# An attention stage with every engine pinned to program order, operands begun three maps ahead, and modulation weights in blocks of 256 features

## The chip, the cores and the metric

The kernel runs on one core of a Trainium2 chip. The metric is the device time of one launch in microseconds, the median of the runs made. A core has five engines that each take their instructions in order: PE (TensorE, matmuls; its weight loads are listed apart as PEld), DVE (VectorE), ACT (ScalarE), POOL (GpSimd) and SP (SyncE, which here only issues DMA transfers). ACT issues a few transfers too.

## What is computed

Two trunk layers over 1152 tokens: 1024 latent tokens and 128 context tokens. Each layer modulates and normalises its input, projects it once, runs four kinds of mixing beside each other, projects the concatenation, and ends with a squared-ReLU MLP:

```python
mod = silu(c) @ ada_w[l] + ada_b[l]              # 6 x 1024 features, for c and for c_ctx
t = mixer_inputs(modulate(x, norm_mix_g, sh1, sc1), lp)
o_a = blocked_attention(...)                     # differential: 4 heads, two maps each, 32-wide q and k
o_a = rmsnorm(o[..., 0, :] - lam * o[..., 1, :], diff_subln_g) * (1 - lam_init)
u   = fourier_mix(t["fnet_u"])
o_c = blocked_attention(...)                     # multi-head latent attention, 4 heads, 96-wide
o_d = blocked_attention(...)                     # grouped queries: 4 q heads, 2 kv heads, 64-wide
x = x + g1 * (concat(o_a, u, o_c, o_d) @ w_out)
x = x + g2 * (square(relu(modulate(x, norm_mlp_g, sh2, sc2) @ mlp_w1)) @ mlp_w2)
```

Latent queries read 1024 latent keys and 128 cached keys in one softmax; context queries read the 128 context keys. All inputs are float32. The kernel keeps that precision by splitting operands into a high and a low part and multiplying the parts.

## The kernel before

**Stages.** Each layer has the same stages in a row: norm and input projection; Fourier mixing, in which the operands of the first attention maps are also read; attention (363 to 871 us in the first layer, 2073 to 2581 us in the second); output projection with the norm before the MLP; and the MLP.

**Maps and pieces.** Attention is 16 maps per layer: maps 0 to 7 differential (two per head), 8 to 11 grouped-query, 12 to 15 latent. `stav` walks a map in ten pieces. For a piece, PE makes scores into a psB buffer (two exist), ACT takes the exponential (L1351) and a float16 copy of it (L1358), POOL subtracts the copy from the exponential for the low part (L294), and `LAG` pieces later PE multiplies the parts by the values into psC. `settle` takes the pieces out of the queue. Beside these matmuls PE makes the row maxima of the following maps (`smax`, into psA, two buffers, reduced by DVE at L1307 and L1312), and the steps of the modulations.

**Operands.** `begin` allocates SBUF pages for a map's operands and issues their loads: for a differential map queries sqr and sqp (96 partitions) and keys sk (97 partitions), for the others gq, gk, mq and mk. There are 44 pages (`NPG`); a load waits until the earlier users of its page are done. Map i+2 is begun when map i starts, its maxima start after those of map i+1 (27 steps, `N_MX`), and `late` loads the second set of operands at column block 5 (`LATE`). When the maxima are known, DVE scales them (L1322), and SP writes the row mr into the last partition of the query tiles by two small transfers (L273).

**Modulations.** `mod_tiles` makes the 6 x 1024 features of ada_w in halves of 512: four loads of ada_p (512 KB each), eight matmuls of 512 columns in two groups, ACT's copy, four matmuls against `quads`, and DVE's additions at L448 and L473. The numbers of steps beside each map are in `MODS`.

**Epilogues.** When a query block's last piece is done, `epi` runs one piece later: DVE divides (L1428 and L1429, or L1437 to L1440). In the second map of a differential head, POOL squares the result (L1502) and DVE sums the squares into dv (L1503); after two heads come the normalisation on POOL and `y_out`, which transposes on PE (L1453), copies on ACT and writes y to DRAM. `y_pairs` reads y back for the output projection and makes high and low parts (L1589, L294).

**What sets the order.** The Tile scheduler orders the instructions of an engine by priorities and expected readiness. Only PE is held to the order in which the attention stage is written (`pin`, while `pinned` is true). DVE, ACT, POOL and SP are ordered by the scheduler, which can also put work of other stages between. Maxima over partitions (`vscale`, `h_scale`) use POOL's `partition_all_reduce`.

## Time and profile before

| | us |
|---|---|
| median of 3 runs | 3513.11 (3511.43 to 3522.86) |
| profiled execution, its own time | 3522.48 |
| its span | 3520.6 |
| PE busy | 3140.4 (89%) |
| DVE busy | 2333.3 (66%) |
| POOL busy | 1486.7 (42%) |
| ACT busy | 1442.1 (41%) |
| mean granted TensorE clock | 0.944 |

The page of the profile shows shares of the span by engine, a strip of 40 slices, the chain of work that ended last, and the costliest groups of instructions. Other views take a stretch of time: the busy time of each engine in it, the list of waits by the instruction that ended them, a timeline of one engine, and the rate of the DMA engines in 40 slices. In the slices the granted clock is 10/10 in the MLP stages and lower in the attention stages.

### The profile page before, as it was taken

To read this page: it belongs to the slowest core of one execution; us is meant where nothing else is said; L and a number is where in the kernel's file an instruction comes from. 1 tells how busy PE (TensorE), PEld (TensorE's weight loads), DVE (VectorE), ACT (ScalarE), POOL (GpSimd) and SP (SyncE) were. 2 spreads that over 40 slices of the span, in tenths; PEclk is the share of its full clock that TensorE was granted. 3 is DMA by queue.
4 is the path that set the end of the run, shared out by engine and by line. 5 is a ranking of instruction groups with operands and counts; after the bars stand their busy time and mean duration, and the time that the engine had idled before them with its cause. 6 is when DMAs were issued, how large, how long until landed. Compare 5 with 4: busy or idle time off the path is not lost.

```text
span 3520.6 us, 59002 instructions
## 1 busy us (share of the span) xinstructions
PE 3140.4 (89%) x23242; PEld 2552.8 (73%) x23242; DVE 2333.3 (66%) x4851; ACT 1442.1 (41%) x2290; POOL 1486.7 (42%) x1146
## 2 busy tenths in 40 slices
PE   7897788988989999999998968887888899999998
PEld 5886566766967777777788856576787776777766
DVE  6865556536377777777687465554446877777776
ACT  4332566745352222222344256665535332222222
POOL 1331576845463323232353146685645422221232
PEclk8998899989999999999999988898999999999999
DMA  6642334434111111111153433433230111111111
GB/s 215 202 145 92 104 123 140 130 113 163 43 49 36 49 49 49 37 48 49 63 183 118 162 94 116 126 112 86 73 132 25 49 48 49 37 49 37 48 37 54
DMA packets 140543, 310.80 MB, mean 88 GB/s; under 512 B 16613, under 2 KB 85682, under 8 KB 140266
## 3 DMA queue, kind: packets, MB, share of 16 engines
q1 hardware_dynamic: 135946, 301.13, 26.6%
q10 hardware_dynamic: 4320, 5.90, 0.5%
q8 instruction: 183, 3.00, 0.4%
q14 instruction: 94, 0.77, 0.1%
HBM read 233.87 MB, written 72.82 MB: 87 GB/s over the span
## 4 chain that ended last, share of the span: by engine, by line
PE 47%; DVE 14%; DMA 13%; issue 11%; POOL 7%; ACT 3%; SPq 1%; POOLq 0%; DVEq 0%; ACTq 0%
PE psD L280 30%; PE psA L280 8%; POOL pg L294 6%; PE psB L280 5%; DVE pg L294 4%; PE psC L280 3%; DMA pg<-sk 2%; DMA pg<-mr 2%; DMA pg<-in_ada_p 2%; DVE pg L1655 2%; DMA pg<-mqp 1%; DMA pg<-sqr 1%; ACT pg L297 1%; SPq L273 1%; DVE pg L1746 1%
## 5 line engine op out<-in xcount | busy, mean ns | idle before, releaser
L280 PE MATMUL psD<-pg,pg 128*128 128x384 f32 (+4 forms) x11173 | 2093.4, 346 | 108.7 <-DVE pg L1784 36.4
L294 POOL TENSOR_TENSOR pg<-pg,pg 128x1024 f16<-128x1024 f32 (+7 forms) x738 | 1216.0, 1663 | 1201.4 <-ACT pg L297 542.4
L280 PEld LDWEIGHTS psD<-pg,pg 128*128 128x128 f32 x8184 | 1422.2, 192 | 77.2 <-DVE pg L294 18.1
L280 PEld LDWEIGHTS <-pg 128*128 128x128 f16 x11448 | 632.3, 101 | 469.0 <-issue 126.0
L1655 DVE SCALAR_TENSOR_TENSOR pg<-psD,mods,pg 128x256 f32<-128x256 f32 (+1 forms) x1088 | 519.5, 511 | 223.0 <-PE psD L280 218.4
L297 ACT ACTIVATE pg<-pg 128x512 f16<-128x512 f32 (+8 forms) x557 | 326.3, 617 | 740.4 <-PE psD L280 312.7
L280 PE MATMUL psA<-pg,pg 128*128 128x128 f16 (+6 forms) x2757 | 497.1, 292 | 92.2 <-DVE mx L1307 19.5
L294 DVE TENSOR_TENSOR pg<-pg,pg 128x384 fp32r<-128x384 f32 (+9 forms) x594 | 472.5, 814 | 62.1 <-ACT pg L297 40.8
L1307 DVE TENSOR_REDUCE mx<-psA 128x1 f32<-128x384 f32 x512 | 281.2, 555 | 273.9 <-PE psA L280 258.6
L1351 ACT ACTIVATE pg<-psB 128x1024 f32<-128x1024 f32 x320 | 301.2, 945 | 267.4 <-PE psB L280 254.9
L280 PE MATMUL psB<-pg,pg 97*128 97x512 f32 (+3 forms) x1064 | 328.8, 425 | 44.2 <-DMA pg<-mr 40.8
L280 PEld LDWEIGHTS psA<-pg,pg 96*128 96x128 f32 (+2 forms) x1377 | 251.4, 205 | 143.0 <-issue 40.0
L280 PE MATMUL psC<-pg,pg 128*128 128x65 f16 (+1 forms) x7008 | 332.9, 200 | 14.0 <-POOL pg L294 13.5
L1358 ACT ACTIVATE pg<-pg 128x1024 f16<-128x1024 f32 x320 | 311.6, 982 | 24.2 <-POOL pg L294 5.7
L280 PEld LDWEIGHTS psB<-pg,pg 97*128 97x128 f32 (+3 forms) x1064 | 201.9, 205 | 86.6 <-issue 55.1
L1312 DVE TENSOR_REDUCE mx<-psA 128x1 f32<-128x384 f32 x256 | 142.0, 555 | 80.8 <-PE psA L280 67.7
L1746 DVE TENSOR_TENSOR pg<-pg 128x512 f32<-128x512 f32 (+2 forms) x192 | 118.6, 632 | 55.3 <-ACT pg L1745 52.1
L1684 POOL PARTITION_ALL_REDUCE wm<-wm x32 | 12.2, 380 | 337.3 <-DVE wm L1683 240.4
L1742 ACT ACTIVATE pg<-pg,wm 128x512 f32<-128x512 f32 x90 | 64.8, 721 | 203.3 <-DVE pg L1793 105.2
L1697 ACT ACTIVATE pg<-pg,wm 128x1024 f32<-128x1024 f32 x32 | 36.9, 1154 | 201.0 <-DVE wm L1953 200.8
L523 ACT ACTIVATE pg<-pg 128x384 f32<-128x384 f32 x120 | 60.8, 521 | 141.2 <-DVE pg L1655 130.9
L811 POOL TENSOR_TENSOR pg<-pg,pg 128x384 f32<-128x384 f32 (+1 forms) x54 | 57.1, 1062 | 111.1 <-ACT pg L297 24.9
(181 smaller groups left out, 1898.9 us busy)
## 6 DMA issues: line engine op xcount, KB each, us to landing
pg<-in_mlp_w SPq DMA_DIRECT2D x128, 512.0 KB
pg<-in_ada_p SPq DMA_DIRECT2D x96, 512.0 KB
pg<-in_w_out SPq DMA_DIRECT2D x16, 512.0 KB
pg<-y_dram SPq DMA_DIRECT2D x42, 192.0 KB
pg<-sk SPq DMA_DIRECT2D x16, 436.5 KB
sqp<-pg SPq DMA_DIRECT2D x36, 192.0 KB
mqp<-pg SPq DMA_DIRECT2D x36, 192.0 KB
pg<-sqp SPq DMA_DIRECT2D x16, 432.0 KB
```

Of the source, the lines that this page charges most:

```text
L280: self.pin(self.nc.tensor.matmul(out, lhsT=lhsT, rhs=rhs, start=start, stop=stop, skip_group_check=skip))
L294: eng.tensor_tensor(out, a, b, ALU.subtract)
L297: self.nc.scalar.activation(out, in_, AF.Copy)
L523: self.nc.scalar.activation(q.t, x, AF.Square)
L811: nc.gpsimd.tensor_tensor(t2.t, s[:, 0:w], tab[0][:, c], ALU.mult)
L1307: nc.vector.reduce_max(mx[:, t, i:i + 1], p[:, 0:TB], axis=AX.X)
L1312: nc.vector.reduce_max(mx[:, t, 2:3], p[:, 128:512], axis=AX.X)
L1351: nc.scalar.activation(e[:, 0:n], src, AF.Exp, scale=M["scale"])
L1358: nc.scalar.activation(pp[:, 0, 0:n], e[:, 0:n], AF.Copy)
L1655: self.nc.vector.scalar_tensor_tensor(xs, o(p), self.mods[:, l, 8 * j + m, s:s + 1], xs, op0=ALU.mult, op1=ALU.add)
L1742: nc.scalar.activation(r.t, src, AF.Relu, scale=W[c][1])
L1746: nc.vector.tensor_tensor(r.t, r.t, r.t, ALU.mult)
```

## The change

Six things change in the attention stage and next to it.

- All five engines are pinned to program order in the attention stage: `pin` adds an order-only dependence between successive instructions of each engine in `PINNED`, after the stage is written.
- Operands are begun three maps ahead: `begin(i+3)` stands after the 30 steps (`N_MX`) of map i+1, instead of `begin(i+2)` ahead of its 27. `leading` also begins map 2. `LATE` is 3 instead of 5, `LAG` 5 instead of 4.
- The row mr is written from ACT's queue (`dma2`), three steps (`ROW_AT`) after DVE has scaled it.
- Modulations are made in quarters of 256 features: two loads of ada_p (128 x 4 x 256, the same bytes each), staged one quarter ahead, eight matmuls of 256 columns, two of `quads`. `MODS` has new numbers of steps.
- `vscale` and `h_scale` use `all_max` (two PE transposes, a DVE maximum and a broadcast copy) instead of POOL's `partition_all_reduce`. Those of the MLP stay.
- `y_pairs` of token blocks 1 and 2 make the high part on ACT, and their DVE instructions stand behind attention's last DVE instruction (`issue_after`).

```diff
-MODS = ((0, 6, 6, 6, 6, 6, 6, 6, 6, 6, 0, 2, 4, 4, 6, 6), (0, 6, 6, 6, 6, 6, 6, 6, 6, 0, 0, 0, 0, 0, 0, 0))
+MODS = ((8, 9, 9, 9, 9, 9, 9, 9, 6, 0, 5, 6, 6, 4, 0, 0), (8, 8, 8, 8, 8, 8, 8, 8, 2, 0, 0, 0, 0, 0, 0, 0))
-LAG = (4, 4, 4)
-N_MX = 27
-LATE = 5
+LAG = (5, 5, 5)
+N_MX, ROW_AT = 30, 3
+LATE = 3
+    def pin(self, first, engines):
+
+        last = {}
+        for i, ins in enumerate(list(self.traced())):
+            if ins.engine in engines:
+                if i >= first and ins.engine in last:
+                    self.tc.add_manual_dep(ins, last[ins.engine].name, NO_SYNC, reason="in order")
+                if i >= first or ins.engine == mybir.EngineType.PE:
+                    last[ins.engine] = ins
...
+        todo = [(j, q) for j in js for q in range(4)]
+        nxt = []
+        yield from self.mod_stage(l, *todo[0], nxt)
+        for i, (j, q) in enumerate(todo):
+            w, nxt = nxt, []
+            if i + 1 < len(todo):
+                yield from self.mod_stage(l, *todo[i + 1], nxt)
             acc = self.ps("A")
-            for g in (0, 2):
-                self.mod_mm(acc, w[g:g + 2], g)
-                self.free(*w[g:g + 2])
-            w = []
-            r = self.t([128, 512])
-            self.acopy(r.t, acc)
+            for g in range(2):
+                self.mod_mm(acc[:, 0:256], w[g], g)
+            self.free(*w)
+            r = self.t([128, 256])
+            self.acopy(r.t, acc[:, 0:256])
...
-    def mod_stage(self, l, j, half, w):
-        for g in range(4):
-            w.append(self.stage(self.I["ada_p"][l, 2 * j + half, g], [128, 2, 512]))
+    def mod_stage(self, l, j, q, w):
+        for g in range(2):
+            w.append(self.stage(self.I["ada_p"][l, 4 * j + q, g], [128, 4, 256]))
             yield
...
+    def all_max(self, src, n):
+
+        nc = self.nc
+        p = self.ps("A")
+        self.mm(p[0:n, 0:128], src, self.ident, True, True)
+        t, b = self.t([n, 128]), self.sm([128, 1], "am", bufs=1)
+        nc.vector.reduce_max(b[0:n], p[0:n, 0:128], axis=AX.X)
+        nc.vector.tensor_copy(t.t, b[0:n].to_broadcast([n, 128]))
+        p = self.ps("A")
+        self.mm(p[:, 0:n], t.t, self.ident[0:n, 0:n], True, True)
+        self.free(t)
+        return p[:, 0:n]
...
         row = M["mrow"][0]
+        for _ in range(ROW_AT):
+            yield
         for q, n in M["mrow"][1:]:
-            self.dma(q.f[row:row + 1, 0:128 * n].rearrange("o (t c) -> o t c", t=n), mr[0:n, :].bitcast(F32))
+            self.dma2(q.f[row:row + 1, 0:128 * n].rearrange("o (t c) -> o t c", t=n), mr[0:n, :].bitcast(F32))
...
         def beside(i):
-            if i + 2 < nm:
-                self.begin(l, i + 2, st, Ms)
             yield from steps(i + 1, N_MX)
+            if i + 3 < nm:
+                self.begin(l, i + 3, st, Ms)
             yield from steps(i + 2, SMX[MAPS[i] // 4])
...
-        self.pinned = False
         while self.late:
             self.tick()
+        self.pin(first, PINNED)
+        self.last_dve = next(i for i in reversed(self.traced()) if i.engine == mybir.EngineType.DVE)
...
-        for b in (1, 2):
-            for _ in self.y_pairs(y, b):
-                pass
+        with self.tc.issue_after(self.last_dve):
+            for b in (1, 2):
+                for _ in self.y_pairs(y, b, True):
+                    pass
...
-        nc.gpsimd.partition_all_reduce(m[:, 3:4], m[:, 2:3], 128, bass_isa.ReduceOp.max)
-        nc.vector.tensor_scalar(m[:, 3:4], m[:, 3:4], 1e-20, None, op0=ALU.max)
+        nc.vector.tensor_scalar(m[:, 3:4], self.all_max(m[:, 2:3], 1), 1e-20, None, op0=ALU.max)
...
-        for i, n in ((0, N_MX), (1, LEAD)):
+        for i, n in ((0, N_MX), (1, LEAD), (2, 0)):
```

Three places show what the pinning and the moves do to the order. The first is SP's queue at the start of the first layer's attention, before (each row is a transfer, destination<-source; sk, sqr and sqp are a map's keys and queries, mr the scaled maxima, in_ada_p modulation weights):

```order
L273 DMA y_dram<-pg_202_3227 128x384
L273 DMA pg_261_3899<-sk_75 97x1152
L273 DMA pg_259_3897<-sqr_71 96x1024
L273 DMA pg_210_3267<-mr_3698 1x8x128
L273 DMA pg_211_3268<-mr_3698 1x9x128
L273 DMA pg_260_3898<-sqp_72 96x1152
L273 DMA pg_262_3907<-in_ada_p 128x1024
L273 DMA pg_265_3963<-in_ada_p 128x1024
```

And the same place after:

```order
L274 DMA pg_250_3681<-in_ada_p 128x1024
L274 DMA pg_259_3782<-sk_75 97x1152
L274 DMA pg_257_3780<-sqr_71 96x1024
L274 DMA pg_258_3781<-sqp_72 96x1152
L274 DMA pg_173_2404<-sk_75 97x128
L274 DMA pg_262_3842<-in_ada_p 128x1024
L274 DMA pg_265_3889<-in_ada_p 128x1024
```

The two rows of mr have left SP's queue. They stand on ACT's queue now, and SP's queue holds loads alone.

The second place is DVE at the end of a differential head in the first layer, before (mx, mm and mr belong to the maxima, ed and er and the row with two psC operands to the epilogue, dv to the sum of squares that POOL makes):

```order
L1437 TENSOR_SCALAR ed_4478<-psC_4266,iunl_3194 128x4
L1316 TENSOR_REDUCE mm_4062<-psA_4466 128x1
L1317 TENSOR_REDUCE mm_4062<-mx_4061 128x8
L1438 RECIPROCAL er_4479<-ed_4478 128x4
L1440 SCALAR_TENSOR_TENSOR pg_193_2980<-psC_4266,er_4479,pg_193_2980 128x64 x4
L1322 TENSOR_SCALAR mr_4490<-psA_4488 9x128
L1437 TENSOR_SCALAR ed_4506<-psC_4494,iunl_3194 128x1
L1307 TENSOR_REDUCE mx_4513<-psA_4515 128x1
L1503 TENSOR_REDUCE dv_3841<-pg_198_3200 128x4
```

And a place of the same kind after:

```order
L1337 TENSOR_REDUCE mm_5079<-mx_5078 128x8
L1342 TENSOR_SCALAR mr_5496<-psA_5494 9x128
L1459 TENSOR_SCALAR ed_5520<-psC_5300,iunl_3238 128x4
L1460 RECIPROCAL er_5521<-ed_5520 128x4
L1462 SCALAR_TENSOR_TENSOR pg_198_3244<-psC_5300,er_5521,pg_198_3244 128x64 x4
L1525 TENSOR_REDUCE dv_3947<-pg_196_3242 128x4
L1459 TENSOR_SCALAR ed_5544<-psC_5530,iunl_3238 128x1
```

The reduction into dv stands directly behind the epilogue that feeds POOL's square, with nothing between. Before, three other instructions stood there.

The third place is POOL there, before (L294 is a piece's low part, L1502 the square of a query block):

```order
L294 TENSOR_TENSOR pg_291_4385<-pg_290_4384,pg_291_4385 128x1024
L294 TENSOR_TENSOR pg_294_4429<-pg_293_4428,pg_294_4429 128x1024
L1502 TENSOR_TENSOR pg_198_3200<-pg_193_2980 128x256
L294 TENSOR_TENSOR pg_297_4474<-pg_296_4473,pg_297_4474 128x1024
```

And after:

```order
L303 TENSOR_TENSOR pg_354_5433<-pg_353_5432,pg_354_5433 128x1024
L303 TENSOR_TENSOR pg_357_5478<-pg_356_5477,pg_357_5478 128x1024
L303 TENSOR_TENSOR pg_360_5516<-pg_359_5515,pg_360_5516 128x1024
L1524 TENSOR_TENSOR pg_196_3242<-pg_198_3244 128x256
L303 TENSOR_TENSOR pg_362_5540<-pg_361_5539,pg_362_5540 128x1024
```

The square stands behind one more low part than before: by the tile numbers (PE's scores, POOL's parts and DVE's epilogue are numbered as they are written), the part ahead of it belongs to the piece that was written just before the epilogue (pg_360_5516, epilogue ed_5520), where before the square ran ahead of the part with the number next below the epilogue's (pg_297_4474, epilogue ed_4478).

## Rows read from the trace of the kernel before

**Rows 1.** Windows, both attention stages: length, busy us (instructions) by engine, clock, DMA share, GB/s.

```profile
363.00:871.00 508.00, 424.57 (x4916) 325.87 (x4916) 288.19 (x642) 319.34 (x362) 339.15 (x227) 0.90 0.43 130
2073.00:2581.00 508.00, 424.03 (x4819) 328.24 (x4819) 282.31 (x624) 317.56 (x358) 339.55 (x227) 0.88 0.35 106
```

**Rows 2.** PE's waits, first layer's attention: what waited, what ended it, us, times, longest.

```profile
PE psB L280 <- DMA pg<-mr: 21.6, 3, 13.2
PE psA L1453 <- DVE pg L1429: 10.3, 2, 7.8
PE psA L280 <- DMA pg<-in_ada_p: 8.9, 6, 3.4
...
PE psA L280 <- DMA pg<-sk: 8.0, 3, 4.4
PE psC L280 <- POOL pg L294: 6.7, 2, 6.2
```

**Rows 3.** PE's waits, second layer's attention.

```profile
PE psB L280 <- DMA pg<-mr: 19.2, 3, 13.1
...
PE psA L280 <- DMA pg<-sqr: 8.1, 3, 4.1
PE psA L1453 <- DVE pg L1429: 7.6, 1, 7.6
PE psA L280 <- DMA pg<-sk: 7.3, 1, 7.3
...
PE psC L280 <- POOL pg L294: 6.8, 2, 6.5
```

**Rows 4.** Chain of waits, first layer: start, us, transfer from its issue to landing.

```profile
380.70 18.39 DMA pg<-mr
...
413.48 22.59 DMA pg<-sk
```

**Rows 5.** PE's timeline behind the wait for mr: start, us, instructions, idle before.

```profile
399.23 1.19 PE L280 MATMUL psB<-pg,pg 97*128 97x512 f32 x2 [13.16 <-DMA pg<-mr]
...
402.96 1.05 PE L280 MATMUL psB<-pg,pg 97*128 97x512 f32 x2
...
405.39 0.63 PE L280 MATMUL psB<-pg,pg 97*128 97x512 f32 x2
```

**Rows 6.** Window just behind that wait, columns as in rows 1.

```profile
399.20:402.00 2.80, 2.77 (x20) 2.19 (x21) 0.56 (x1) 1.40 (x2) 0.00 (x0) 0.50 0.52 192
```

**Rows 7.** DMA rate from 380 to 400 us, in 40 slices of 0.5 us.

```profile
GB/s 28 28 92 134 331 230 72 51 129 249 404 267 272 330 370 346 379 182 167 158 331 330 125 35 28 28 28 18 28 28 28 28 28 28 18 33 18 52 159 246
```

**Rows 8.** The page's list of DMA issues: transfer, queue, count, KB each.

```profile
pg<-sk SPq DMA_DIRECT2D x16, 436.5 KB
```

**Rows 9.** POOL's timeline behind h_scale's maximum over partitions.

```profile
580.76 8.78 POOL L294 TENSOR_TENSOR pg<-pg,pg 128x1024 f16<-128x1024 f32 x5 [7.39 <-issue]
```

**Rows 10.** Timelines of POOL, DVE and PE at an epilogue of the first layer.

```profile
424.68 0.62 POOL L1502 TENSOR_TENSOR pg<-pg 128x256 f32<-128x256 f32 x1
426.30 2.13 POOL L294 TENSOR_TENSOR pg<-pg,pg 128x1024 f16<-128x1024 f32 x1 [1.01 <-ACT pg L1358]
...
425.33 0.42 DVE L1503 TENSOR_REDUCE dv<-pg 128x4 f32<-128x256 f32 x1 [1.57 <-POOL pg L1502]
...
426.27 0.50 PE L280 MATMUL psA<-pg,pg 96*128 96x256 f32 x2 [1.63 <-DVE mx L1307]
```

**Rows 11.** DVE's waits, first layer's attention: us, times, longest.

```profile
DVE dv L1503 <- POOL pg L1502: 13.1, 10, 2.1
```

**Rows 12.** The page's groups: busy, mean ns of one, idle before.

```profile
L1351 ACT ACTIVATE pg<-psB 128x1024 f32<-128x1024 f32 x320 | 301.2, 945 | 267.4 <-PE psB L280 254.9
...
L1358 ACT ACTIVATE pg<-pg 128x1024 f16<-128x1024 f32 x320 | 311.6, 982 | 24.2 <-POOL pg L294 5.7
```

**Rows 13.** PE's waits in the two MLP stages, first layer, then second.

```profile
PE psD L280 <- DVE pg L1784: 5.6, 4, 2.2
...
PE psD L280 <- DVE pg L1784: 30.7, 13, 3.4
```

More of the change, by code (lines that the diff above doesn't have):

```diff
@@ L36 @@
 S_GQA = 64 ** -0.5
+NO_SYNC = mybir.DependencyInfo(mybir.DependencyClass.NoSync, mybir.DependencyReason.DATA)
+PINNED = tuple(getattr(mybir.EngineType, e) for e in ("PE", "SP", "Activation", "DVE", "Pool"))
 NPG = 44
@@ L279, in mm, with traced @@
     def mm(self, out, lhsT, rhs, start, stop, skip=False):
-        self.pin(self.nc.tensor.matmul(out, lhsT=lhsT, rhs=rhs, start=start, stop=stop, skip_group_check=skip))
-    def pin(self, ins):
-        if self.pinned:
-            self.tc.keep_in_program_order(ins)
+        self.nc.tensor.matmul(out, lhsT=lhsT, rhs=rhs, start=start, stop=stop, skip_group_check=skip)
+    def traced(self):
+        return self.nc.cur_bb.bb.instructions
+    def pin(self, first, engines):
[6 more added lines that the diff above has]
+                    last[ins.engine] = ins
     def mm3(self, out, ah, al, bh, bl, start, stop, skip=False):
@@ L488, in mod_first @@
             for j in range(2):
-                w = []
-                for g in range(4):
-                    w.append(self.stage(self.I["ada_p"][0, 2 * j + half, g], [128, 2, 512]))
-                    if g % 2:
-                        self.mod_mm(acc[j], w, g - 1)
-                        self.free(*w)
-                        w = []
-                    yield
+                for q in range(2):
+                    for g in range(2):
+                        w = self.stage(self.I["ada_p"][0, 4 * j + 2 * half + q, g], [128, 4, 256])
+                        self.mod_mm(acc[j][:, 256 * q:256 * q + 256], w, g)
+                        self.free(w)
+                        yield
             p = self.ps("A")
@@ L906, in vscale @@
         m2 = self.sm([128, n], "vm2")
-        nc.gpsimd.partition_all_reduce(m2, m1, 128, bass_isa.ReduceOp.max)
-        nc.vector.tensor_scalar(m2, m2, 1e-30, None, op0=ALU.max)
+        nc.vector.tensor_scalar(m2, self.all_max(m1, n), 1e-30, None, op0=ALU.max)
         sc = self.sm([128, n], "vsc" + tag)
@@ L1452, in y_move @@
         for j in range(self.nj(b)):
[L1453 removed]
+            nc.tensor.transpose(pt[:, 128 * j:128 * j + 128], src[:, j, :], self.ident)
         self.free(src)
@@ L1529, in attention @@
         nm = len(MAPS)
-        self.pinned = True
+        first = len(self.traced())
         def steps(i, n):
@@ L1577, in begin, with y_pairs @@
         M["gen"], M["done"] = self.smax(M), 0
-    def y_pairs(self, y, b):
+    def y_pairs(self, y, b, late=False):
         ys = [self.t([128, TB]) for _ in ORDER_Y[:-1]]
@@ L1588, in y_pairs @@
             p = self.pair()
-            self.nc.vector.tensor_copy(p.h, s.t)
+            if late:
+                self.acopy(p.h, s.t)
+            else:
+                self.nc.vector.tensor_copy(p.h, s.t)
             self.sub(self.nc.vector, p.l, s.t, p.hf)
@@ L2136, in _arrays @@
     a["cols"] = cols
-    a["ada_p"] = i["ada_w"].reshape(L, 4, 2, 128, 12, 512).transpose(0, 4, 1, 3, 2, 5)
+    a["ada_p"] = i["ada_w"].reshape(L, 2, 4, 128, 24, 256).transpose(0, 4, 1, 3, 2, 5)
     a["ada_b"] = i["ada_b"].reshape(L, 48, 128).transpose(0, 2, 1)
```

19 lines of the change are left out of this document (6 added, 13 removed).

## The prediction

> **What bounds the kernel now.** PE is busy for 89% of the span, so the first view is the windows by stage: they show where PE is not busy. Both attention stages are 508 us long with 424.57 and 424.03 us of PE work, so 83.4 and 84.0 us are idle there, and the granted clock is 0.90 and 0.88 [rows 1]. The next busiest engine is POOL at 339 us: no engine but PE is near full, and the losses are waits. The second view is the list of PE's waits. In the first layer five groups hold 55.5 us of the 83.4: mr 21.6, the last epilogue 10.3, ada_p 8.9, sk 8.0, POOL's low part 6.7 [rows 2]. In the second they are mr 19.2, sqr 8.1, the last epilogue 7.6, sk 7.3, POOL 6.8 [rows 3], 49.0 of 84.0. Transfers hold 38.5 and 34.6 us of these. The rest, some 28 and 35 us, is mostly short waits for DVE's maxima.
>
> The third view is the chain of waits, which says why the transfers are late. A few KB of mr took 18.39 us from issue to landing, and PE stood still for 13.16 us [rows 4, 5]. The DMA rate shows what was moving: 28 GB/s in the first slices and again at the end, hundreds between [rows 7]. The 28 GB/s is what a load of sk gets; its 436.5 KB [rows 8] take 447 thousand bytes / 28 = 16 us, and from issue to landing it was 22.59 [rows 4].
>
> The fourth view is the clock. Behind the 13.16 us of idle, PE ran at the low level (0.50, that is 1.2 GHz) [rows 6]. Two 512-column matmuls took 1.05 us there against 0.63 later [rows 5], so 40% of such time is lost. The slow rows run from 399.2 to about 403.8, 4.6 us: such a gap costs 1.8 us more after it has ended. After a gap of 1.63 us the next two matmuls took 0.50 us, no longer than at full speed [rows 10]: that gap cost only itself.
>
> **The change part by part.** The sum is made against the profiled execution, 3522.48 us (span 3520.6); that is 9.4 us over the median, 3513.11.
>
> Loads one map earlier, mr on ACT's queue, ada_p one quarter ahead. By the two orders, pages were allocated four to five pieces before first use and now are ten to eleven. A map of ten pieces is 508 / 16 = 31.8 us, so the lead grows from some 14 to some 33 us, against 22.59 us for the slowest load [rows 4]. The row mr no longer stands on SP behind loads that wait for pages, and is used some seven pieces after it is written in the new order, 22 us against 18.39. This takes away up to the 38.5 + 34.6 = 73.1 us. What may stay: sk still takes 16 us, and the other bytes of a map, 130 GB/s x 31.8 = 4.1 MB less 0.45 [rows 1, 8], spread over 16 DMA engines at about 28 GB/s each, come to 8 us on the same engine. That is 24 us for each differential map, and a map with no idle time at full clock needs about as long. So I take three quarters: -55 us (ends 0 and -73).
>
> The clock. The waits for transfers, POOL and the last epilogue number 16 and 10 [rows 2, 3]; at most a dozen of them are over 3 us, and at 1.8 us each they give back 22 us. Gaps that follow one another may have held the clock low for longer: 0.10 and 0.12 of 508 us at half speed means 102 and 122 us at the low level [rows 1], of which the 167 us of idle can hold all but 57, and 40% of 57 to 224 is 23 to 90 us. I take -38 us, some two fifths of the upper end.
>
> `all_max` in place of POOL's maximum. POOL did nothing for 7.39 us behind it [rows 9], and PE waited 6.2 and 6.5 us [rows 2, 3]. The new chain is two small matmuls and two DVE steps whose result is needed in a later stage: -13 us. The ones of `vscale` stand in front of attention; I set them at nothing, because the Fourier stage's transfers are late there too.
>
> The tail. The last epilogue was late by 10.3 and 7.6 us [rows 2, 3], since DVE first did copies of `y_pairs`. Now these stand behind it, but the output projection then waits for 14 pairs in a row. Half is given back later: -9 us (ends -18 and +10).
>
> Quarters of modulations. Sixteen matmuls of 256 columns take the place of eight of 512. By the rows they are 0.25 us [rows 10] and 0.315 each [rows 5], 1.5 us more for 512 features; twenty such halves lie in the two stages, 30 us at most, nothing at least as the columns are the same. The rows overlap, so I take 0.3 each: +6 us. DVE's and ACT's doubled small steps go between the maxima in program order, and an ACT copy can hold a psA buffer while ACT finishes a piece; forty of them at 0 to 2 us (0.945 + 0.982 [rows 12]), I take 0.25 each: +10.
>
> Program order on DVE and POOL. This is the price. The sum of squares into dv stands right behind the epilogue, and POOL's square behind the low part of the piece just scored (the second and third order places). So DVE waits until PE's score (0.63), exponential and copy (0.945, 0.982), low part (2.13), square (0.62) are through, and adds its own 0.42: 5.7 us [rows 5, 10, 12]. Behind it on DVE are the maxima, on which PE's two psA buffers hang; PE has work for about 2 us, so a gap of 3.5 us. Before, it was ten waits of 13.1 us in all [rows 11], such as the gap of 1.63 [rows 10]. There are 4 odd maps x 3 blocks x 2 layers = 24. Twenty-four times 3.5 - 1.6 is +46 us; at 24 x (3.5 + 1.8), with the clock, it would be +89, and where POOL is ahead, 0. I take 46.
>
> SP and ACT in order: SP's queue holds loads that each wait for a page; in order, none can pass another. I set it at nothing while the lead covers it; without that cover the transfer term above shrinks. LAG 5 adds a piece of slack to POOL and ACT: nothing by itself.
>
> The MLP stages change only as the scheduler lays out DVE anew. PE waits for L1784 5.6 us in one layer and 30.7 in the other [rows 13]: -25 to +25, I take 0.
>
> Sum: -55 - 38 - 13 - 9 + 6 + 10 + 46 = -53 us in the two stages as taken. The short waits for DVE's maxima outside epilogues (63 us with both layers) shrink too as maxima run three more steps ahead and PE has a fifth piece of scores to multiply; I take a third, -20. So -73: 3522.48 - 73 = 3449.5, and with the 9.4 us between this execution and the median, **3440 us**.
>
> **Rivals.** *All waits go.* Transfers 73, clock 60, POOL 13, tail 18, the maxima's waits 20, and dv's wait is hidden by the fifth piece; +6: -178, or about 3335 at best; with a little of each left, 3370. For it: the lead exceeds the slowest load. Against it: POOL's order.
>
> *The loads stay late.* The one slow lane for sk stays, and mr stays behind its packets. Then 40.8 us of mr and its clock (6 waits x 1.8 = 11) come back: 3440 + 52 = 3492. For it: 24 us of one lane per map against some 25 of PE. Against it: the lead. The Trainium skill ("DMA: Bandwidth & Descriptors", section "Issuing engines are not separate DMA queues") says that transfers issued from SP and ACT run on the same 16 DMA engines, and that issuing from a second engine saves only issue time. By that rule the move of mr from SP to ACT alone would return nothing of its 18.39 us, and only the later use would hide it; no row before shows ACT's queue under this load.
>
> *Slower.* One mechanism: DVE blocked at each of the 24 sums of squares for the whole 5.7 us chain with nothing behind it done, because the pieces stand in order on ACT and POOL too. 24 x (5.7 + 1.8 - 1.1) = +154, against gains of 55 + 38 + 13 + 9, and +16 for modulations: +55, less the 20 of maxima: 3548. It decides when PE's work behind the epilogue falls below about 1 us. For it: the order. Against it: psA's two buffers and five pieces of values.
>
> *Nothing.* The pages (44) fill: three maps hold them, SP in order waits for each page as long as before, and only POOL and tail are won, given back at dv: 3505 to 3520.
>
> **How the numbers follow.** Forecast 0.52 (3400 to 3475), all waits go 0.14, loads late 0.14, slower 0.13, nothing 0.07. Faster by over 0.3% (which is about what a measurement can tell from no change) is then 0.80, within it 0.07, slower 0.13. The range leaves out most of the slower case and the extreme of the best: 3360 to 3525.
>
> **What would show it.** Right: no wait of PE for mr or ada_p over 3 us in either stage; no POOL gap behind a maximum; a clock above 0.93 in attention; PE waits that end with a maximum queued behind DVE's sum of squares, 24 of 3 to 4 us. Wrong: sk or mr still high in PE's list; attention stages longer than 508 us; DVE waiting for squares for over 100 us; or a MLP stage that moved by more than 25 us, which nothing here prices.

## The result

The changed kernel is slower: a median of 3596.28 us (3583.99 to 3604.06) against 3515.9 for the kernel before in the same comparison, a ratio of 1.022 with a 95% interval of 1.0203 to 1.0237. The profiled execution has a span of 3598.2 us; that of the kernel before had 3520.6.

To see where the 77.6 us between the two spans lie, the trace is cut at the start of PE's first score (psB) and of its last weighted sum (psC) in each attention stage. The last row ends with PE's last matmul, 7 us ahead of the end of either span. All runs of this study are cut in the same way below.

| stretch, us | before | after | difference |
|---|---|---|---|
| ahead of the first attention | 363.1 | 368.5 | +5 |
| attention, first layer | 505.1 | 567.9 | +63 |
| from there to the second attention | 1204.8 | 1231.0 | +26 |
| attention, second layer | 505.6 | 517.8 | +12 |
| behind it | 934.7 | 905.8 | -29 |

The two stretches that hold the MLPs nearly cancel (+26 and -29), so the loss is in attention. The windows of the two stages after the change (length, busy us and instructions of PE, PEld, DVE, ACT and POOL, granted clock, DMA share, GB/s):

```profile
368.00:936.00 568.00, 463.88 (x5100) 356.70 (x5100) 283.34 (x633) 327.12 (x380) 336.83 (x226) 0.84 0.34 104
2167.00:2685.00 518.00, 434.36 (x4939) 341.75 (x4940) 266.17 (x608) 324.31 (x374) 336.90 (x226) 0.87 0.33 101
```

Against [rows 1], PE is busy 39 and 10 us longer and the clock is lower, 0.84 for 0.90 and 0.87 for 0.88. Matmul time at the low level (1.2 GHz) is 144 and 111 us, added up over all rows of the two stages; before it was 69 and 97. At the 40% that the prediction found lost at that level, the 89 us more cost an estimated 36.

PE's waits in the first layer's attention, after the change (what waited and what ended it: us, times, longest):

```profile
PE psA L281 <- DVE mx L1327: 40.3, 40, 5.2
PE psB L281 <- ACT pg L1373: 19.4, 2, 13.1
PE psA L281 <- ACT pg L306: 12.4, 4, 8.9
...
PE psA L281 <- DMA pg<-in_ada_p: 2.6, 2, 2.4
...
PE psB L281 <- DMA pg<-mr: 2.1, 1, 2.1
```

And in the second layer's:

```profile
PE psA L281 <- DVE mx L1327: 30.0, 37, 5.1
PE psA L281 <- ACT pg L306: 15.3, 10, 6.9
PE psB L281 <- ACT pg L1373: 13.5, 3, 6.7
...
PE psB L281 <- DMA pg<-mr: 1.8, 2, 1.2
```

The transfers that headed [rows 2, 3] are gone or nearly so: mr went from 40.8 us to 3.9, sk and sqr no longer stand in the list. In their place stand DVE's maxima and ACT's exponentials and copies, 131 us for both layers. The loads came in time, and PE now waits for engines. The first of these entries was much shorter before, in the first and the second layer:

```profile
PE psA L280 <- DVE mx L1307: 8.6, 11, 1.9
...
PE psA L280 <- DVE mx L1307: 9.9, 11, 2.5
```

Two places show why. The first is an epilogue at 448 us, in the timelines of DVE, POOL and PE (start, us, instructions, idle before and what ended it):

```profile
447.80 0.86 DVE L1462 SCALAR_TENSOR_TENSOR pg<-psC,er,pg 128x64 f32<-128x64 f32 x4
453.45 0.42 DVE L1525 TENSOR_REDUCE dv<-pg 128x4 f32<-128x256 f32 x1 [4.79 <-POOL pg L1524]
453.79 0.55 DVE L1327 TENSOR_REDUCE mx<-psA 128x1 f32<-128x384 f32 x1
...
448.08 2.13 POOL L303 TENSOR_TENSOR pg<-pg,pg 128x1024 f16<-128x1024 f32 x1 [1.03 <-ACT pg L1380]
450.73 2.12 POOL L303 TENSOR_TENSOR pg<-pg,pg 128x1024 f16<-128x1024 f32 x1 [0.52 <-ACT pg L1380]
452.81 0.61 POOL L1524 TENSOR_TENSOR pg<-pg 128x256 f32<-128x256 f32 x1
...
454.39 0.80 PE L281 MATMUL psA<-pg,pg 96*128 96x256 f32 x2 [5.14 <-DVE mx L1327]
454.99 0.88 PE L281 MATMUL psC<-pg,pg 128*128 128x65 f16 x12
```

Read it upwards: PE waits 5.14 us for a maximum, the maximum stands behind DVE's sum of squares, that waits 4.79 us for POOL's square, and POOL first makes two low parts, each of which waited for ACT's copy. Afterwards PE is at the low clock level: 0.50 is granted from 454.3 to 458 us. Before, the same kind of place cost 1.63 us of PE [rows 10]. Over the whole run DVE's waits for squares were, before and after the change:

```profile
DVE dv L1503 <- POOL pg L1502: 25.8, 20, 2.1
...
DVE dv L1525 <- POOL pg L1524: 81.4, 24, 5.8
```

The second place is at 746 us, in the timelines of ACT and PE:

```profile
745.85 0.26 ACT L306 ACTIVATE pg<-psA 128x128 f32<-128x128 f32 x1
762.68 0.33 ACTq L278 DMA_DIRECT2D y_dram<-pg  x1
763.06 1.02 ACT L1373 ACTIVATE pg<-psB 128x1024 f32<-128x1024 f32 x1 [16.95 <-DMA pg<-mqr]
...
764.14 2.07 PE L281 MATMUL psB<-pg,pg 128*128 128x512 f32 x4 [13.15 <-ACT pg L1373]
```

ACT has made its copy at 746.1 and next issues the store of y. That store is not issued until 762.68, and the profile names the landing of a load of mqr, a transfer of SP's, as what ended the wait. The exponentials behind the store wait too, and PE stands still for 13.15 us. The store needs no byte of mqr. The trace tells what ties the two together: each transfer raises a semaphore (a counter that others can wait for) when it has landed, and the store of 762.68 and the mqr load that SP issued at 740.91 have the same one, number 101. ACT waits for that number ahead of the store.

### The profile page after: what moved, and what is told of

It reads as the page before. It is cut to its first block, busy times and chain, and to the rows that moved or that the text cites. A ratio compares the mean times of both kernels' runs of the same rounds, so it can differ in the third digit from the quotient of the medians.

```text
span 3598.2 us, 59901 instructions
## 1 busy us (share of the span) xinstructions
PE 3204.3 (89%) x23650; PEld 2603.2 (72%) x23650; DVE 2296.0 (64%) x4887; ACT 1462.6 (41%) x2338; POOL 1478.6 (41%) x1140
## 5 line engine op out<-in xcount | busy, mean ns | idle before, releaser
L281 PE MATMUL psD<-pg,pg 128*128 128x384 f32 (+3 forms) x11129 | 2091.4, 346 | 91.5 <-DVE pg L1811 22.4
L303 POOL TENSOR_TENSOR pg<-pg,pg 128x1024 f16<-128x1024 f32 (+8 forms) x741 | 1212.9, 1648 | 1522.5 <-ACT pg L306 609.1
L281 PE MATMUL psA<-pg,pg 128*128 128x128 f16 (+7 forms) x2746 | 524.8, 302 | 139.4 <-DVE mx L1327 67.5
L306 ACT ACTIVATE pg<-pg 128x512 f16<-128x512 f32 (+9 forms) x585 | 339.6, 612 | 735.3 <-PE psD L281 292.2
L303 DVE TENSOR_TENSOR pg<-pg,pg 128x512 f16<-128x512 f32 (+12 forms) x607 | 467.8, 786 | 96.7 <-ACT pg L306 75.9
L1327 DVE TENSOR_REDUCE mx<-psA 128x1 f32<-128x384 f32 x512 | 282.1, 555 | 259.9 <-PE psA L281 245.5
L281 PEld LDWEIGHTS psA<-pg,pg 96*128 96x128 f32 (+2 forms) x1377 | 265.6, 216 | 199.4 <-DVE mx L1327 86.3
L281 PE MATMUL psB<-pg,pg 97*128 97x512 f32 (+3 forms) x1064 | 342.1, 439 | 41.8 <-ACT pg L1373 32.9
L281 PE MATMUL psC<-pg,pg 128*128 128x65 f16 (+1 forms) x7008 | 341.7, 204 | 8.5 <-POOL pg L303 5.5
L281 PEld LDWEIGHTS psB<-pg,pg 97*128 97x128 f32 (+3 forms) x1064 | 211.7, 215 | 73.1 <-ACT pg L1373 36.6
L1773 DVE TENSOR_TENSOR pg<-pg 128x512 f32<-128x512 f32 (+2 forms) x192 | 122.6, 651 | 81.4 <-ACT pg L1772 79.8
L306 ACT ACTIVATE pg<-psD 128x384 f32<-128x384 f32 (+3 forms) x104 | 54.7, 532 | 126.7 <-PE psD L281 123.2
```

The costliest lines, as they stand in the source:

```text
L281: self.nc.tensor.matmul(out, lhsT=lhsT, rhs=rhs, start=start, stop=stop, skip_group_check=skip)
L303: eng.tensor_tensor(out, a, b, ALU.subtract)
L306: self.nc.scalar.activation(out, in_, AF.Copy)
L1327: nc.vector.reduce_max(mx[:, t, i:i + 1], p[:, 0:TB], axis=AX.X)
L1773: nc.vector.tensor_tensor(r.t, r.t, r.t, ALU.mult)
```

## The experiments

Each run is told as its ratio to the kernel before, timed on the same chip. The changed kernel's is 1.022. The stretches come from one profiled execution of each run. By their intervals, two ratios have to differ by about 0.003 (10 us) to be told apart.

| run | median us | ratio (95% interval) | attention 1, 2, us | between, behind, us |
|---|---|---|---|---|
| only PE pinned (`e_pin_pe`) | 3467.54 | 0.9861 (0.984 to 0.9881) | 481.5, 471.8 | 1235.4, 905.6 |
| sum of squares later (`e_dv_later`) | 3552.96 | 1.01 (1.0074 to 1.0126) | 536.0, 498.8 | 1228.6, 904.9 |
| no transfer from ACT (`e_no_act_dma`) | 3542.08 | 1.0067 (1.0049 to 1.0086) | 541.9, 492.7 | 1230.6, 901.8 |
| before, all pinned (`e_before_pin5`) | 3543.76 | 1.0082 (1.0061 to 1.0104) | 530.6, 515.2 | 1197.2, 931.3 |
| both single edits (`e_dv_act`) | 3502.04 | 0.994 (0.992 to 0.996) | 517.5, 469.2 | 1231.9, 904.9 |
| PE pinned, two maps ahead (`e_pe_two_maps`) | 3493.16 | 0.9911 (0.9885 to 0.9938) | 523.6, 444.2 | 1230.2, 906.0 |
| PE pinned, mr from SP (`e_pe_mr_sp`) | 3506.76 | 0.9951 (0.9935 to 0.9967) | 521.4, 471.7 | 1231.5, 904.2 |
| PE pinned, h_scale on POOL (`e_hmax_pool`) | 3485.35 | 0.9888 (0.9867 to 0.9909) | 500.1, 480.4 | 1225.0, 905.0 |
| PE pinned, three maps, then two (`e_mix`) | 3442.5 | 0.9789 (0.9775 to 0.9804) | 487.6, 440.3 | 1232.9, 906.8 |
| PE pinned, two maps, map 2 early (`e_two_lead`) | 3482.41 | 0.9902 (0.9887 to 0.9917) | 524.1, 438.9 | 1233.1, 911.4 |
| three then two, y stored from SP (`e_mix_y_sp`) | 3443.06 | 0.979 (0.9769 to 0.9811) | 477.4, 444.9 | 1232.3, 912.7 |
| PE pinned, halves of 512 (`e_halves`) | 3459.19 | 0.9828 (0.9804 to 0.9851) | 454.5, 452.2 | 1251.3, 910.3 |
| all but ACT pinned (`e_pin_no_act`) | 3603.79 | 1.0248 (1.0228 to 1.0268) | 550.5, 521.4 | 1236.3, 916.4 |
| all but DVE pinned (`e_pin_no_dve`) | 3543.63 | 1.0079 (1.0057 to 1.0101) | 537.2, 499.5 | 1224.1, 904.9 |
| three then two, halves (`e_mix_halves`) | 3432.13 | 0.9758 (0.9734 to 0.9781) | 450.9, 449.8 | 1233.0, 906.7 |
| the same, map 2 not early (`e_mix_halves_m2`) | 3442.65 | 0.979 (0.9772 to 0.9808) | 457.4, 440.6 | 1233.3, 907.7 |

### Is it the order?

```diff
-PINNED = tuple(getattr(mybir.EngineType, e) for e in ("PE", "SP", "Activation", "DVE", "Pool"))
+PINNED = tuple(getattr(mybir.EngineType, e) for e in ("PE",))
```

> The changed kernel with only PE pinned to program order; SP, ACT, DVE and POOL are ordered by the scheduler as before the change. Theory (program order on the other four engines costs the time, by DVE standing behind POOL's squares and ACT behind its own transfers): the earlier loads pay and nothing takes it back, 3440 to 3500 us, DVE's waits for squares near 25 us in both layers instead of 81. Rival (what is new in content costs: quarters of modulations, five pieces of lag, three maps of pages): still 3570 to 3600 us.

Measured: 3467.54 us, 126 us under the changed kernel by the ratios (1.022 - 0.9861 of 3515) and 1.4% under the kernel before. Its windows in attention, and DVE's waits for squares over the run:

```profile
367.00:849.00 482.00, 433.21 (x5105) 336.97 (x5106) 284.55 (x634) 320.86 (x383) 336.82 (x226) 0.91 0.41 125
2084.00:2556.00 472.00, 409.06 (x4944) 323.20 (x4944) 270.30 (x608) 313.97 (x373) 336.31 (x226) 0.92 0.37 109
```

```profile
DVE dv L1525 <- POOL pg L1524: 17.9, 19, 2.0
```

The content of the change pays, and pinning the four other engines takes more back. The shift between the two MLP stretches (+30 and -29) is still there, so it does not come from the pinning.

The other direction is the kernel before with the order alone added: the pinning of PE is taken out of `mm` and `pin`, and the changed kernel's `pin` is called behind the attention stage.

```diff
-        self.pinned = True
+        first = len(self.traced())
...
-        self.pinned = False
         while self.late:
             self.tick()
+        self.pin_all(first, PINNED)
```

> The kernel before with nothing changed but that all five engines are pinned to program order in the attention stage. Theory (the order itself costs): 60 to 130 us slower than before, 3575 to 3645 us, with DVE's waits for squares at 60 us or more. Rival (the order costs only together with the other changes): within 15 us of before.

Measured: 3543.76 us, 0.8% or 29 us slower than before, which neither theory gave. Its waits for squares:

```profile
DVE dv L1517 <- POOL pg L1516: 50.2, 24, 4.2
```

So the order costs on its own, but only 29 us. With the other changes on top it costs 126. The trace shows less of both stalls here: 50.2 us of waits for squares where the changed kernel has 81.4, and 20 us that ACT stands ahead of a transfer for the semaphore of an earlier one, where the changed kernel, which also issues mr from ACT, has 73 (waits of over 1 us in the two stages).

### DVE behind POOL's squares

```diff
-                nc.vector.reduce_sum(st["dv"][:, 4 * b:4 * b + n, h % 2], s.t, axis=AX.X)
-                self.free(s)
+                dv = st["dv"]
+
+                def squares():
+                    nc.vector.reduce_sum(dv[:, 4 * b:4 * b + n, h % 2], s.t, axis=AX.X)
+                    self.free(s)
+                self.defer(1, squares)
...
-                step()
+                self.defer(1, step)
```

> The changed kernel, with DVE's sum of squares written one piece later than POOL's square. Theory (DVE's 24 waits for squares make most of PE's new gaps): the waits fall from 81 us to under 15, and 40 to 70 us come back, 3525 to 3555 us. Rival (these waits are covered, or another engine in order is late next): under 15 us come back.

Measured: 3552.96 us, 42 us back by the ratios, within the theory's range. The waits fell by half and not to 15:

```profile
DVE dv L1528 <- POOL pg L1524: 39.9, 16, 5.3
```

One piece later is not late enough everywhere, because POOL's square itself is late behind low parts: the epilogue that waited 4.79 us in the lines above still waits 4.33, with the square behind two of them. All but DVE pinned asks the same of the order:

```diff
-PINNED = tuple(getattr(mybir.EngineType, e) for e in ("PE", "SP", "Activation", "DVE", "Pool"))
+PINNED = tuple(getattr(mybir.EngineType, e) for e in ("PE", "SP", "Activation", "Pool"))
```

> The changed kernel with PE, SP, ACT and POOL pinned, DVE ordered by the scheduler. Theory (DVE's order costs the waits for squares and little else): 40 to 75 us faster than the changed kernel, 3520 to 3555 us, DVE's waits for squares under 40 us. Rival (POOL's order makes the squares late whatever DVE does first): under 20 us faster.

Measured: 3543.63 us, 50 us back. DVE's waits for squares and ACT's longest wait there:

```profile
DVE dv L1525 <- POOL pg L1524: 27.9, 17, 3.4
```

```profile
ACT pg L1373 <- DMA pg<-mqr: 16.9, 1, 16.9
```

DVE's order is worth 42 to 50 us, by two different edits: the first moves the sum of squares and the step that uses it, the second frees all of DVE. The stall of ACT is untouched by either.

### ACT behind its own transfers

```diff
-            self.dma2(q.f[row:row + 1, 0:128 * n].rearrange("o (t c) -> o t c", t=n), mr[0:n, :].bitcast(F32))
+            self.dma(q.f[row:row + 1, 0:128 * n].rearrange("o (t c) -> o t c", t=n), mr[0:n, :].bitcast(F32))
...
-        self.dma2(self.y_dram[k, :, 512 * b:512 * b + n], o.t)
+        self.dma(self.y_dram[k, :, 512 * b:512 * b + n], o.t)
```

> The changed kernel, with mr and the stores of y issued from SP instead of ACT. Theory (ACT in order is held by transfers that it issues, 37 us in the first layer at mq loads and 34 in the second): these waits vanish and 20 to 45 us come back, 3550 to 3575 us. Rival (SP in order then holds its loads behind mr and the stores): PE waits for sk, mr or ada_p again, 0 to 60 us more, 3600 to 3660 us.

Measured: 3542.08 us, 54 us back, more than expected. The waits for ACT's exponential left PE's list of the first layer; in their place came part of what the rival gave:

```profile
PE psA L281 <- DVE mx L1327: 36.9, 31, 5.4
PE psA L281 <- DMA pg<-in_ada_p: 17.6, 3, 6.8
```

Is it ACT's order, or that ACT issues at all?

```diff
-PINNED = tuple(getattr(mybir.EngineType, e) for e in ("PE", "SP", "Activation", "DVE", "Pool"))
+PINNED = tuple(getattr(mybir.EngineType, e) for e in ("PE", "SP", "DVE", "Pool"))
```

> The changed kernel with PE, SP, DVE and POOL pinned, ACT ordered by the scheduler. Theory (ACT's order costs what its transfers make it wait, DVE's order the rest): 45 to 75 us faster than the changed kernel, 3520 to 3550 us, DVE's waits for squares still about 80 us. Rival (the scheduler's ACT order can't help while DVE and POOL are pinned): under 25 us faster.

Measured: 3603.79 us, no gain; the rival holds. ACT's list in the first layer, ordered by the scheduler, still has the same entry:

```profile
ACT pg L1373 <- DMA pg<-mqr: 17.0, 1, 17.0
```

So the theory that ACT's own order costs falls. What the waits have in common is the semaphore. SP's and ACT's 1086 transfers share eight of them, and 1036 wait for their own one before they are issued, which is until the transfer that had it before has landed. In the changed kernel's two stages ACT stands for over 1 us ahead of 13 of its transfers, and at 11 of them what ends the wait is that its own semaphore was raised by a load that SP had issued: 73 us in all, 41 ahead of stores of y and 31 ahead of mr.

Nor does it take the pinning of SP. With only PE pinned the first layer has 1.2 us of waits for mqr, but the second layer still has the stall, mostly ahead of mr. PE's wait there and ACT's:

```profile
PE psB L281 <- ACT pg L1373: 23.1, 4, 11.1
...
ACT pg L1380 <- DMA pg<-mk: 16.1, 2, 9.1
ACT pg L1373 <- DMA pg<-mr: 14.4, 1, 14.4
```

So the pinning makes the stall larger, but by the trace its source is that ACT issues transfers that share semaphores with SP's loads. That transfers taken off ACT give the 54 us back is shown by the run; a kernel with semaphores of their own for ACT's transfers was not run.

### Do the two add up?

The kernel has the diffs of `e_dv_later` and `e_no_act_dma`, the two edits of the sections above.

> The changed kernel, all five engines pinned, with both single edits together: the sum of squares one piece later, and no transfer issued from ACT. Theory (two separate stalls): the two gains add, 43 + 54 us, 3485 to 3515 us. Rival (one hides behind the other): under 75 us come back, 3520 to 3545 us.

Measured: 3502.04 us. By ratios the two edits give 1.2% and 1.5%, together 2.8%: they add, and the kernel with all five engines pinned is then 0.6% faster than before. PE's waits in the first layer that remain:

```profile
PE psA L281 <- DVE mx L1327: 24.2, 34, 4.4
PE psA L281 <- DMA pg<-in_ada_p: 21.5, 6, 11.4
```

98 of the 126 us are so accounted for. The last 28, against PE alone pinned, lie in the first layer: its attention is 36 us longer (517.5 for 481.5), the second's 3 shorter. With PE alone pinned the same two lines are:

```profile
PE psA L281 <- DVE mx L1327: 14.2, 31, 1.7
...
PE psA L281 <- DMA pg<-in_ada_p: 6.2, 2, 3.8
```

So squares that are still late (10 us more) and loads of ada_p on SP's queue, which now also has mr and the stores (15 us more), are the largest part that can be named. How the 28 us divide stays open.

### What pays in the content

With PE alone pinned, single parts were undone. First the maps ahead:

```diff
         def beside(i):
+            if i + 2 < nm:
+                self.begin(l, i + 2, st, Ms)
             yield from steps(i + 1, N_MX)
-            if i + 3 < nm:
-                self.begin(l, i + 3, st, Ms)
...
-LATE = 3
+LATE = 5
...
-        for i, n in ((0, N_MX), (1, LEAD), (2, 0)):
+        for i, n in ((0, N_MX), (1, LEAD)):
```

> The kernel with only PE pinned, with operands begun two maps ahead at a map's start as before the change (and the second set at block 5); everything else as in the changed kernel. Theory (the earlier loads are what pays there): 25 to 55 us slower than with three maps, 3490 to 3520 us, and PE waits for sk or sqr again by 15 us or more. Rival (the gain is the mr row's and the quarters' alone): within 12 us, 3455 to 3480 us.

Measured: 3493.16 us, 18 us slower by the ratios (0.9911 against 0.9861), under the theory's range, and it divides: the first layer is 42 us longer, the second 28 us shorter. PE's waits in the first layer, from just ahead of its attention stage:

```profile
PE psA L281 <- DMA pg<-sqr: 29.9, 2, 22.9
...
PE psA L281 <- DMA pg<-sk: 16.2, 3, 7.3
```

The wait of 22.9 us ended 14 us before the first score; it lengthens the stretch ahead of the stage (380.8 us), and the others lie in the stage. Three maps help the first layer and harm the second, where they came with the 23.1 us of waits for ACT's exponentials. Taking three in the first layer and two in the second:

```diff
         def beside(i):
+            if l == 1 and i + 2 < nm:
+                self.begin(l, i + 2, st, Ms)
             yield from steps(i + 1, N_MX)
-            if i + 3 < nm:
+            if l == 0 and i + 3 < nm:
                 self.begin(l, i + 3, st, Ms)
...
-            if t == LATE and "late" in M:
+            if t == M["late_at"] and "late" in M:
...
+        M["late_at"] = (LATE, 5)[l]
...
-        for i, n in ((0, N_MX), (1, LEAD), (2, 0)):
+        for i, n in ((0, N_MX), (1, LEAD), (2, 0))[:3 - l]:
```

> The kernel with only PE pinned; operands three maps ahead in the first layer, two maps ahead (second set at block 5) in the second, whose attention stage took 444 us with two and 472 with three. Theory (three maps hold pages and DMA slots so that ACT waits in the second layer): 15 to 30 us faster than with three in both, 3437 to 3455 us. Rival (the 444 us came with an order that only the two-map program of both layers has): 3460 to 3475 us.

Measured: 3442.5 us, as the theory had it, 2.1% faster than before. PE's waits for ACT's exponentials are gone from its list of the second layer. Beginning map 2 early with two maps in both layers does not do the same:

```diff
         def beside(i):
+            if i + 2 < nm and not (l == 0 and i == 0):
+                self.begin(l, i + 2, st, Ms)
             yield from steps(i + 1, N_MX)
-            if i + 3 < nm:
-                self.begin(l, i + 3, st, Ms)
...
-LATE = 3
+LATE = 5
...
-        for i, n in ((0, N_MX), (1, LEAD), (2, 0)):
+        for i, n in ((0, N_MX), (1, LEAD), (2, 0))[:3 - l]:
```

> The kernel with only PE pinned; two maps ahead in both layers, but map 2 of the first layer is begun ahead of the attention stage, as in the changed kernel. Theory (with two maps the first layer lost its time to one load of 22.9 us at its start): the first stage falls from 524 to under 500 us, 3440 to 3470 us. Rival (the later maps' loads are late too): 3475 to 3495 us.

Measured: 3482.41 us, 0.9902; the first layer's attention stayed at 524 us, the rival's result. The load of 22.9 us, which the theory put at the start of that stage, lay ahead of it: there the stretch fell from 380.8 to 366.6 us. Then mr's queue:

```diff
-            self.dma2(q.f[row:row + 1, 0:128 * n].rearrange("o (t c) -> o t c", t=n), mr[0:n, :].bitcast(F32))
+            self.dma(q.f[row:row + 1, 0:128 * n].rearrange("o (t c) -> o t c", t=n), mr[0:n, :].bitcast(F32))
```

> The kernel with only PE pinned, with mr issued from SP's queue as before the change, still three steps later. Theory (mr stood behind loads that wait for pages on SP): PE waits for mr again, 10 to 30 us slower, 3478 to 3498 us. Rival (the later use hides mr wherever it is issued, and ACT is free of its waits): 0 to 15 us faster, 3452 to 3468 us.

Measured: 3506.76 us, 0.9% or 32 us slower, at the theory's upper end and over it. PE's waits in the first and second layer:

```profile
PE psB L281 <- DMA pg<-mr: 43.1, 6, 19.6
```

```profile
PE psB L281 <- DMA pg<-mr: 24.3, 6, 7.4
```

The move of mr to ACT's queue is what frees it; the later use alone does not hide it. The theory's reason does not hold, though. In the trace, mr is issued as soon from SP as from ACT (2.3 and 2.8 us behind DVE's result, in the mean of both layers). It is late after that: from the end of its issue to landing it takes 8.4 us in the mean and 18.9 at most from SP's queue, where the loads are, and 3.4 and 7.2 from ACT's. All of the loss is in the first layer (521.4 us for 481.5). In the second the 24.3 us cost nothing in sum (471.7 for 471.8): there ACT, which no longer issues mr, holds PE for 10.6 us instead of 23.1:

```profile
PE psB L281 <- ACT pg L1373: 10.6, 3, 8.8
```

For the stores of y, the queue does not matter once only PE is pinned:

```diff
-        self.dma2(self.y_dram[k, :, 512 * b:512 * b + n], o.t)
+        self.dma(self.y_dram[k, :, 512 * b:512 * b + n], o.t)
```

> e_mix with the stores of y issued from SP instead of ACT; mr stays on ACT. Theory (the stores hold ACT while they wait for the transfer that used their slot before): PE's waits for ACT's exponential fall by 10 us or more, 5 to 20 us faster than e_mix. Rival (freed of the pinning, ACT is not held): within 5 us, or slower as SP's loads stand behind the stores.

Measured: 3443.06 us, the same as without the edit; the rival. Then the maximum over partitions:

```diff
-        nc.vector.tensor_scalar(m[:, 3:4], self.all_max(m[:, 2:3], 1), 1e-20, None, op0=ALU.max)
+        nc.gpsimd.partition_all_reduce(m[:, 3:4], m[:, 2:3], 128, bass_isa.ReduceOp.max)
+        nc.vector.tensor_scalar(m[:, 3:4], m[:, 3:4], 1e-20, None, op0=ALU.max)
```

> The kernel with only PE pinned, with h_scale's maximum over partitions on POOL again (vscale's stay on PE and DVE). By the order its MLP stages get DVE orders that neither kernel had. Theory (the MLP stages' shift of +30 us in the first layer and -29 us in the second hangs on these two instructions): the stretch between the two attention stages and the one behind the second move by 10 us or more each, and PE waits some 6 us behind POOL's maximum in each layer. Rival (the shift comes from elsewhere): both stretches stay within 5 us of 1235 and 906 us.

Measured: 3485.35 us, 0.27% or 9 us slower, which is within the noise of the two ratios. PE's waits for POOL's low part are back in both layers:

```profile
PE psC L281 <- POOL pg L303: 7.9, 3, 5.9
```

```profile
PE psC L281 <- POOL pg L303: 7.7, 2, 6.5
```

The stretch between the attention stages moved by 10 us, the one behind by 1. Without this edit the same stretch is 1224.1 us in one run and 1236.3 in another, so even the 10 us need not be h_scale's. The cause of the MLP stretches' shift stays open. Last the quarters, put back to halves of 512 features with four loads and the old numbers of steps (`mod_tiles`, `mod_stage`, `mod_mm`, `MODS` and the layout of ada_p as they were):

```diff
-        todo = [(j, q) for j in js for q in range(4)]
+        todo = [(j, half) for j in js for half in range(2)]
...
-        for g in range(2):
-            w.append(self.stage(self.I["ada_p"][l, 4 * j + q, g], [128, 4, 256]))
+        for g in range(4):
+            w.append(self.stage(self.I["ada_p"][l, 2 * j + half, g], [128, 2, 512]))
```

> The kernel with only PE pinned, with the modulations in halves of 512 features, four loads each, and the old numbers of steps, as before the change. Theory (the quarters cost matmuls and small steps but bring their loads earlier): PE waits for ada_p 10 us or more again; within 15 us of 3467 us. Rival (quarters are the larger cost): 15 to 30 us faster.

Measured: 3459.19 us, 12 us faster by the ratios, just over the noise and within the theory's range. Its windows in attention:

```profile
383.00:837.00 454.00, 419.05 (x4905) 322.07 (x4904) 260.65 (x599) 317.54 (x371) 336.45 (x226) 0.94 0.44 132
2088.00:2541.00 453.00, 403.65 (x4818) 316.90 (x4819) 257.89 (x591) 313.51 (x365) 336.22 (x226) 0.92 0.39 115
```

Both attention stages are shorter, by 47 us together, and the stretches ahead of each longer, by 31: PE waits there for one load of sqr, 20.5 and 19.5 us. Next are the halves with three maps in the first layer and two in the second, that is this diff on top of the one of `e_mix`:

> e_mix with the modulations in halves of 512 features, as before the change. Theory (the quarters cost attention some 40 us, and the late load belongs to the three maps begun ahead): the second layer's late load is gone, 3400 to 3430 us. Rival (halves bring a late load in any order): 3435 to 3460 us.

Measured: 3432.13 us, 0.9758, 11 us faster than `e_mix`, a little over the theory's range and the fastest of all. The second layer's late load is gone (the stretch between is back to 1233.0 from 1251.3); the first's is not:

```profile
PE psA L281 <- DMA pg<-sqr: 20.5, 1, 20.5
```

The last run takes map 2's early start away from this kernel:

```diff
-            if l == 1 and i + 2 < nm:
+            if (l == 1 or i == 0) and i + 2 < nm:
                 self.begin(l, i + 2, st, Ms)
...
-        for i, n in ((0, N_MX), (1, LEAD), (2, 0))[:3 - l]:
+        for i, n in ((0, N_MX), (1, LEAD)):
```

> e_mix_halves, with map 2 of the first layer begun when the attention stage starts instead of ahead of it. Theory (its loads stand on SP ahead of those that the first maxima need): PE's wait of 20 us for sqr ahead of the first stage vanishes, 10 to 25 us faster than e_mix_halves unless map 2's own loads are late. Rival (the wait for sqr comes from other loads): within 8 us.

Measured: 3442.65 us, 11 us slower by the ratios. The named wait vanished, but PE stood still for 33.4 us at the same place and the profile names nothing for it. What delays the stage ahead of the first attention stays open.

## Why the prediction was wrong

The prediction was 3440 us, faster; the result is 3596, slower, 156 us apart. About half of this is the price of the order: 46 us were taken, 126 measured. The other half is the gain of the rest: 119 us were taken, 48 measured with only PE pinned. Point by point:

- **Loads.** Right: PE's waits for mr, ada_p, sk and sqr fell from the 73 us named to under 10 for both layers together, more than the 55 us taken. So the rival "the loads stay late" did not come true; with mr on SP's queue it would have in part, by the 32 us of `e_pe_mr_sp`. The Trainium skill, cited there ("DMA: Bandwidth & Descriptors", section "Issuing engines are not separate DMA queues"), says that transfers from SP and ACT share the same 16 DMA engines, so that a second issuing engine saves only issue time. For this small row the trace does not agree: it is issued no sooner from ACT, but lands in 3.4 us in the mean where it took 8.4 from SP's queue.
- **Program order on DVE.** Right in mechanism: forecast +46, measured 42 to 50. That the sizes meet is partly luck. Forecast were 24 gaps of 3.5 us; in the trace nine of PE's waits for a maximum are over 3 us, of 4.6 to 5.7 us, four more are about 2.6, and behind the one shown above the granted clock is 0.50.
- **SP and ACT in order, "at nothing".** This is the step that failed. Transfers issued from ACT cost 54 us there. The prediction weighed what is queued behind SP's loads, and not that a transfer on ACT can be held until a load of SP's with the same semaphore has landed, with all of ACT's instructions that stand behind it, exponentials among them. It is not a matter of order alone: with only PE pinned the second layer still has this stall. Another 28 us of the order's price were not divided.
- **The clock.** Wrong in sign: forecast -38, and about +36 by the same 40% (89 us more at the low level). With only PE pinned the matmul time at the low level is 80 and 61 us, 25 less than before, which gives back an estimated 10. It was a term that could only follow the gaps, and the gaps grew.
- **Quarters.** Forecast +16 for both terms, and in total they cost 12. The place is another: put back to halves, the attention stages alone are 47 us shorter, and a load that then comes late ahead of each stage takes 31 of them back.
- **Maxima.** Forecast -20 from the three steps more ahead; wrong in sign. PE's waits for L1327 (L1307 before) rose from 18.5 to 70.3 us in the two stages, mostly as the last link of DVE's chain; with only PE pinned they are 33, still more than before.
- **POOL's maximum and the tail.** The waits behind both are gone. For h_scale's move 13 us were taken; the 9 us measured are within the noise.
- **The MLP stretches.** They moved by +26 and -29 us, each just past the 25 us that the prediction would allow without a cause; their sum is near zero as taken. No run shows the cause.

With PE alone pinned there is no price of the order, and the parts that the prediction summed (-55 - 38 - 13 - 9 + 6 + 10 - 20 = -119) gave -48. Of the 71 us missing, 25 are the second layer's third map (`e_mix` against `e_pin_pe`, 0.72%), with which PE's 23.1 us of waits for ACT go. The terms of the clock (28 short) and of the maxima (over 20 short) are the others that are known to be too large; the three overlap, and how the 71 us divide was not settled. The slower rival named DVE's chain as the one mechanism, and that is not enough. Without a transfer from ACT, but with the chain, the pinned kernel is still 0.67% slower than before: there the chain and the undivided 28 us outweigh the 48 us gained. ACT's stall is the rest of the loss.

## What to carry to other kernels

An engine that is pinned to the order in which the code is written holds, at every wait, all that is written behind it. Before pinning, look for instructions that are written right behind the request they depend on (the sum behind another engine's square) and for transfers issued by a compute engine, and move those first. Where a transfer is issued late with its data ready, look in the trace for the semaphore that it waits for and for the transfer that used it before. And test an order and a content that come in one change apart: here the one costs 3.6% and the other gains 1.4%.

## What was not expected of the hardware

A store issued by ACT stood for 16.9 us until a load issued by SP had landed, with its own data ready, and held ACT's exponentials all that time. It did so under two different orders of ACT (16.9 and 17.0 us), and cost PE 13.15 us in one place. The reason is in the program and not in the chip: both transfers were given one semaphore.

The small row mr landed 8.4 us after its issue in the mean, and 18.9 at most, when it was issued from the queue that also has the loads, and 3.4 and 7.2 us when it was issued from ACT's.
